# A SwiGLU trunk on one core: the forms of x moved beside the second chunk, and every sum of weight quarters on VectorE

## The chip, the cores and the metric

The kernel runs on one core of a Trainium2 chip. The metric is device time in microseconds (us), the median of several runs. A profiled execution of the kernel is there beside the times; its records show what each engine did and when.

## The reference

Two layers, 256 tokens, width 1024, inner width of an FFN 2816, all in float32. What matters here is the FFN, of which there are four (two in each layer); between them stand a mixer of three attention branches and a small gated input.

```python
def swiglu(x, w1, w3, w2):
    return (jax.nn.silu(x @ w1) * (x @ w3)) @ w2
...
    for i in range(DEPTH):
        h = h + 0.5 * swiglu(rms_norm(h, g_ffn1[i]), w1_a[i], w3_a[i], w2_a[i])
        u = rms_norm(h, g_mix[i])
        h = h + hybrid_mixer(u, w_in[i], ...)
        h = h + 0.5 * swiglu(rms_norm(h, g_ffn2[i]), w1_b[i], w3_b[i], w2_b[i])
        ple_gate = jax.nn.sigmoid(rms_norm(h, g_ple[i]) @ w_ple_gate[i])
        h = h + ple_gate * (p[i] @ w_ple_proj[i])
    return rms_norm(h, g_final)
```

## The kernel before

**Arithmetic.** TensorE multiplies operands in a rounded float32 form. Each float32 tile is therefore split into a rounded part "hi" and the rest "lo": ScalarE casts the hi part (line 135 for a tile, line 86 in `load`), VectorE subtracts it from the tile to get lo (lines 136 and 87), and each product is three matmuls, hi by hi, lo by hi and hi by lo (`mm3`, lines 102 to 104). In an FFN a weight tile is 128x1024 (512 KB), and a matmul of it is 128x128 by 128x512. So each tile of weights costs one cast on ScalarE and one subtraction on VectorE before TensorE can start on it.

**An FFN.** The inner width is cut into 11 chunks of 256 columns of w1 and 256 of w3. `up(c)` makes a chunk for both blocks of 128 tokens (`tb`), with 48 matmuls; `gated` turns the result into silu(x w1)*(x w3), a tile `pr` of 128x256 (ScalarE makes `act`, VectorE multiplies, line 238); `turn(c)` transposes `pr` on TensorE into `ffT` (fhi, flo); `down(c, j)` multiplies it with w2 into four banks `acc`. Chunks 0 and 1 are made first. Chunks 2, 3 and 4 are made in quarters (`up_unit`), spread between other work. Chunks 5 to 10 are made in pairs, (5,6), (7,8) and (9,10).

**A pair.** A pair is a product of a matrix of 2x2 blocks of x with one of 2x2 blocks of weights, made from seven block products in the place of eight. For that it needs sums of the blocks of x and sums of the blocks of weights:

- `x_forms`, once in an FFN: VectorE adds hi and lo of the four blocks of x (line 293), scales the second token block with `rb` (line 297; `rb` is a ratio of the two norms, brought to all partitions by a matmul with ones, line 274, and copied by ScalarE, line 276), makes the sums (lines 284 and 305) and splits five of them (tiles `q`). That is 15 VectorE operations of 128x512 beside three small ones.
- `pair(c)`: the four weight quarters x, y, w, z, each two tiles `wr` of 128x1024 that `fetch` loads through SyncE's queue. `form(i)` makes the sums in place: x+=w, x+=z and y+=x by VectorE (`add`, line 330), w+=z by an accumulating transfer that GpSimd issues and that reads z again from memory (`plus`, line 334). `make(i)` splits a quarter or a sum. `products()` yields the seven products in the order 1, 2, 5, 3, 6, 7, 4, each of 12 matmuls, with VectorE's sums of the results between (line 356, names m, u, v and c); a product has a bank `tr` of the two that there are, and the next product that wants the bank waits until it has been read.

`block` runs a plan: "S" is one product of the pair (with the splits and sums that the next ones need), "P" a quarter of an ordinary chunk, "D" a unit of `down`, "T" a `turn`. While one pair runs, the next pair's quarters are fetched, and its first product's tiles are split.

**Order.** A scheduler puts the instructions in order when the kernel is built; every engine then runs its own queue strictly in order, and waits at an instruction whose operands are late, with all that stands behind it. Before the change, the beginning of an FFN is written as up(0), up(1), then `x_forms`, the fetches of pair (5,6), turn(0), the splits for product 1 and the pair's plan, which begins with product 1. The first FFN differs: its first chunk is loaded together with x, and its norms are computed while chunk 1 runs.

Of the kernel before, what the change touches and what calls it, by code (L numbers as in the profile page):

```python
# [11 lines left out]
ALU = mybir.AluOpType  # L12
PSUM = bass.MemoryType.PSUM

P = 128
L = 2
S = 256
TB = S // P
D = 1024
# [14 lines left out]
def trunk(ctx: ExitStack, tc: tile.TileContext, a: dict, out: bass.AP):  # L34
    nc = tc.nc
# [13 lines left out]
    def const(name, shape):  # L49
        t = cp.tile(shape, F32, tag=name, name=name)  # L50
        tc.keep_in_program_order(nc.sync.dma_start(t, a[name]))
        return t
# [22 lines left out]
    def load(src, n=U, pool=None, step=U):  # L75
        raw = wp.tile([P, U], F32, tag="raw", name=nm("raw"), bufs=4)
        if pool is None:
            hi = wp.tile([P, U], F32R, tag="whi", name=nm("whi"), bufs=7)
            lo = wp.tile([P, U], F32R, tag="wlo", name=nm("wlo"), bufs=7)
        else:  # L80
            hi = pool.tile([P, U], F32R, tag="whi", name=nm("whi"), bufs=4)
            lo = pool.tile([P, U], F32R, tag="wlo", name=nm("wlo"), bufs=4)
        for i in range(0, n, step):
            c = slice(i, min(i + step, n))
            nc.sync.dma_start(raw[:, c], src[:, c])
            A.copy(hi[:, c], raw[:, c])  # L86
            V.tensor_tensor(out=lo[:, c], in0=raw[:, c], in1=hi[:, c].bitcast(F32), op=ALU.subtract)  # L87
        return hi, lo
# [26 lines left out]
    def bank_acc():  # L115
        return bank("acc", 4)
# [74 lines left out]
    def ffn(li, w13, w2, r, g, first=False, aside=None):  # L191
        nonlocal ident
        with tc.tile_pool(name=nm("fp"), bufs=3) as fp:
# [7 lines left out]
            if first:  # L201
                un0 = start(wtile)
            acc = []
            ffT = {}
            prs = {}

            def up(c, un, bank):
                os = []
                for tb in range(TB):
                    o = bank()  # L210
                    for kt in range(KT):
                        w = [x[:, (kt % 2) * 512 : (kt % 2) * 512 + 512] for x in un[kt // 2]]
                        mm3(o, x_at(tb, kt), w, kt == 0, kt == KT - 1)
                        if kt == 1:
                            settle()
                    os.append(o)
                    if r is not None:
                        gated(c, tb, o, r[tb])
                return os


# [12 lines left out]
            def gated(c, tb, o, scale):  # L234
                act = fp.tile([P, FC], F32, tag="act", name=nm("act"), bufs=2)
                A.activation(act, o[:, :FC], AF.Silu, scale=scale)
                pr = fp.tile([P, FC], F32, tag="pr", name=nm("pr"), bufs=6)
                V.scalar_tensor_tensor(
                    out=pr, in0=o[:, FC:], scalar=scale, in1=act, op0=ALU.mult, op1=ALU.mult
                )  # L240
                prs[c, tb] = pr

            def turn(c):
                fhi = fp.tile([P, 2, S], F32R, tag="fhi", name=nm("fhi"), bufs=4)
                flo = fp.tile([P, 2, S], F32R, tag="flo", name=nm("flo"), bufs=4)
                ffT[c] = (fhi, flo)
                t = bank_tr()
                for tb in range(TB):
                    for j in range(2):
                        PE.transpose(  # L250
                            t[:, j * S + tb * P : j * S + (tb + 1) * P], prs[c, tb][:, j * P : (j + 1) * P], ident
                        )
                split_T(t.rearrange("p (j t) -> p j t", j=2), fhi, flo)
# [61 lines left out]
            def pair(c, bank):  # L315
                t = {q: [wtile() for _ in range(2)] for q in "xywz"}
                fw = {}
                quarters = {"x": (0, 0), "y": (1, 0), "w": (0, 1), "z": (1, 1)}

                def at(q, u):  # L320
                    kh, nh = quarters[q]
                    return w13[li, c + nh, 2 * kh + u]

                def fetch(q):
                    for u in range(2):
                        nc.sync.dma_start(t[q][u], at(q, u))

                def add(q, other):
                    for u in range(2):
                        V.tensor_tensor(out=t[q][u], in0=t[q][u], in1=t[other][u], op=ALU.add)  # L330

                def plus(q, other):
                    for u in range(2):
                        nc.gpsimd.dma_start(t[q][u], at(other, u), accum_op=ALU.add)


                def form(i):
                    if i == 1:
                        add("x", "w")
                    elif i == 2:  # L340
                        add("x", "z")
                    elif i == 3:
                        plus("w", "z")
                    else:
                        add("y", "x")

                def make(i):
                    fw[i] = [split_w(w) for w in t[{1: "x", 2: "y", 5: "x", 3: "z", 6: "x", 7: "w", 4: "y"}[i]]]

                def product(o, i, start=False):  # L350
                    for kt in range(4):
                        m = [y[:, (kt % 2) * 512 : (kt % 2) * 512 + 512] for y in fw[i][kt // 2]]
                        mm3(o, [y[:, kt, :] for y in fx[i]], m, start and kt == 0, kt == 3, skip_group_check=True)

                def sum_(out, a, b, op=ALU.add):
                    V.tensor_tensor(out=out, in0=a, in1=b, op=op)


                def products():
                    o = bank()  # L360
                    product(o, 1, True)
                    m1 = t512("m1")
                    A.copy(m1, o)
                    yield
                    product(o, 2)
                    gated(c, 0, o, r[0])
                    yield
                    o = bank()
                    product(o, 5, True)
                    c5 = t512("c5")  # L370
                    A.copy(c5, o)
                    yield
                    product(o, 3)
                    v = t512("v")
                    A.copy(v, o)
                    yield
                    o = bank()
                    product(o, 6, True)
                    u2 = t512("u2")
                    sum_(u2, o, m1)  # L380
                    sum_(v, v, u2, ALU.subtract)
                    gated(c + 1, 0, v, r[0])
                    yield
                    product(o, 7)
                    sum_(m1, o, m1)
                    sum_(c5, c5, m1, ALU.subtract)
                    gated(c + 1, 1, c5, r[0])
                    yield
                    o = bank()
                    product(o, 4, True)  # L390
                    sum_(m1, o, m1)
                    gated(c, 1, m1, r[0])
                    yield

                return make, fetch, form, products()


# [33 lines left out]
                        turn(*arg)  # L431
                return following

            for c in range(2):
                if first and c == 1:

                    un = []
                    for i in range(4):
                        un.append(load(w13[li, c, i]))
                        if i < 2:  # L440
                            load_h(i)
                    ident = const("ident", [P, P])
                    r = [norm_r(tb) for tb in range(TB)]
                    for tb, o in enumerate(os0):
                        gated(0, tb, o, r[tb])
                    up(c, un, bank_acc)
                else:
                    os0 = up(c, un0 if first and c == 0 else [load(w13[li, c, i]) for i in range(4)], bank_mm)
                if c == 1:
                    acc.extend(bank_acc() for _ in range(4))  # L450
                    fx = x_forms()
                    wg = pair(5, bank_tr)
                    for q in "xywz":
                        wg[1](q)
                if c >= 1:
                    turn(c - 1)
            wg[0](1)
            if first:
                later()
            wg = block(wg, [  # L460
                ("S",), ("P", 2, 0), ("D", 0, 0), ("S",), ("P", 2, 1), ("S",), ("D", 0, 1), ("P", 2, 2), ("S",),
                ("T", 1), ("P", 2, 3), ("S",), ("D", 1, 0), ("S",), ("D", 1, 1), ("S",), ("T", 2),
            ], (7, bank_tr))
            wg = block(wg, [
# [576 lines left out]
    def load_h(tb):  # L1041
        tc.keep_in_program_order(nc.sync.dma_start(h[tb], a["x"][tb * P : (tb + 1) * P, :]))
# [8 lines left out]
    r = None  # L1051
    for li in range(L):
        g = [gcol[:, li, j, :] for j in range(4)]
        r = ffn(li, a["w13a"], a["w2a"], r, g[1], first=li == 0)
# [90 lines left out]
```

## Time and profile before

| what | value |
|---|---|
| median of 3 runs | 1357.7 us (1357.37 to 1358.7) |
| the profiled execution, its own time | 1355.51 us |
| its span in the trace | 1353.7 us |
| mean granted TensorE clock | 0.985 |
| TensorE (PE) busy | 1308.6 us, 97% of the span |
| VectorE (DVE) busy | 1042.0 us, 77% |
| ScalarE (ACT) busy | 837.2 us, 62% |
| GpSimd (POOL) busy | 69.5 us, 5% |

PEld in the profile is TensorE's loading of weights, which runs beside its matmuls. SPq and POOLq are the queues from which SyncE and GpSimd issue transfers. A row of a timeline gives a start, a duration, the engine, the line of the kernel, the operation, what it writes and reads, the shape, how many instructions lie in the row, and in brackets how long the engine had been idle and what ended that. The four FFNs begin at about 15, 460, 680 and 1130 us of the span, and run for some 180 us each.

### The profile page before, as it was taken

The page shows a single profiled execution, that of the slowest core. Times are in us where ns is not written, and L with a number is a line of the kernel's source. Part 1 is how long each engine was busy: PE and PEld are TensorE (multiplying, and loading weights), DVE is VectorE, ACT ScalarE, POOL GpSimd, SP SyncE. Part 2 cuts the span into 40 slices and gives each one's busy share as a digit, 9 for nine tenths or more (in the row PEclk, how much of TensorE's full clock was granted, in tenths as well). Part 3 has the DMA queues.
Part 4 walks back from the last instruction along what each step waited for, and adds up shares of the span by engine and source line. Part 5 has one row for each costly group of instructions (what it writes and reads, how often), then busy time and mean ns, then how long its engine had stood idle before and what let it go on. Part 6 is the DMA issues. An engine that isn't in the chain of part 4 may idle for free.

```text
span 1353.7 us, 18041 instructions
## 1 busy us (share of the span) xinstructions
PE 1308.6 (97%) x6576; PEld 1093.2 (81%) x6576; DVE 1042.0 (77%) x1466; ACT 837.2 (62%) x1257; POOL 69.5 (5%) x133
## 2 busy tenths in 40 slices
PE   8899999999999979999979999999999999799997
PEld 6688889978888858888858888898888788688886
DVE  6998875666768689897769988666666675998875
ACT  5666556665775456665746666566667744666655
POOL 1000000001100000000100000000010000000000
PEclk9899999999999989999999999999999999899999
DMA  8975457433546568555568744473444466675552
GB/s 306 314 251 156 139 164 222 167 125 126 169 143 186 190 211 276 187 147 180 170 219 273 234 121 150 147 225 134 156 145 136 157 187 241 210 236 160 155 169 81
DMA packets 71225, 249.21 MB, mean 184 GB/s; under 512 B 8544, under 2 KB 9184, under 8 KB 71136
## 3 DMA queue, kind: packets, MB, share of 16 engines
q1 hardware_dynamic: 67104, 234.39, 51.1%
q0 software_dynamic: 3456, 12.58, 5.5%
q8 instruction: 51, 0.84, 0.2%
q10 hardware_dynamic: 576, 1.08, 0.2%
q14 instruction: 38, 0.31, 0.1%
HBM read 246.98 MB, written 1.05 MB: 183 GB/s over the span
## 4 chain that ended last, share of the span: by engine, by line
PE 91%; DVE 5%; issue 1%; ACT 1%; DMA 1%; SPq 0%; POOLq 0%; POOL 0%; ACTq 0%
PE mm L102 15%; PE mm L104 14%; PE mm L103 14%; PE acc L103 8%; PE acc L104 8%; PE acc L102 8%; PE tr L103 6%; PE tr L102 5%; PE tr L104 5%; PE tr L250 1%; PE tr L150 1%; DVE q L136 1%; DVE wlo L136 1%; PE tr L742 1%; DVE wlo L87 1%
## 5 line engine op out<-in xcount | busy, mean ns | idle before, releaser
L87 DVE TENSOR_TENSOR wlo<-raw,whi 128x1024 fp32r<-128x1024 f32 (+1 forms) x346 | 411.4, 1200 | 93.1 <-ACT whi L86 90.8
L86 ACT CAST whi<-raw 128x1024 fp32r<-128x1024 f32 (+1 forms) x346 | 354.3, 1033 | 165.7 <-PE acc L104 52.3
L102 PE MATMUL mm<-whi,xhi 128*128 128x512 f32 (+1 forms) x632 | 247.1, 396 | 0.0
L104 PE MATMUL mm<-whi,xlo 128*128 128x512 f32 (+1 forms) x632 | 245.8, 389 | 0.0
L103 PE MATMUL mm<-wlo,xhi 128*128 128x512 f32 (+1 forms) x632 | 245.6, 389 | 0.0
L135 ACT CAST whi<-wr 128x1024 fp32r<-128x1024 f32 (+1 forms) x176 | 179.9, 1032 | 93.2 <-PE acc L104 53.1
L136 DVE TENSOR_TENSOR wlo<-wr,whi 128x1024 fp32r<-128x1024 f32 (+1 forms) x176 | 207.4, 1198 | 25.7 <-ACT whi L135 24.5
L104 PEld LDWEIGHTS mm<-whi,xlo 128*128 128x128 f32 x632 | 118.7, 188 | 24.8 <-DVE xlo L136 0.7
L102 PEld LDWEIGHTS mm<-whi,xhi 128*128 128x128 f32 x632 | 118.7, 188 | 24.4 <-DVE sqk L542 0.7
L104 PE MATMUL acc<-whi,flo 128*128 128x512 f32 x352 | 137.6, 391 | 0.0
L103 PEld LDWEIGHTS mm<-wlo,xhi 128*128 128x128 f32 x632 | 118.9, 188 | 23.1 <-DVE wlo L136 0.2
L103 PE MATMUL acc<-wlo,fhi 128*128 128x512 f32 x352 | 137.1, 390 | 0.0
L102 PE MATMUL acc<-whi,fhi 128*128 128x512 f32 x352 | 135.2, 392 | 0.0
L102 PE MATMUL tr<-whi,q 128*128 128x512 f32 x240 | 94.1, 392 | 0.0
L104 PE MATMUL tr<-whi,q 128*128 128x512 f32 x240 | 93.6, 390 | 0.0
L103 PE MATMUL tr<-wlo,q 128*128 128x512 f32 x240 | 93.4, 389 | 0.0
L330 DVE TENSOR_TENSOR wr<-wr,wr 128x1024 f32<-128x1024 f32 x72 | 86.3, 1222 | 0.0
L104 PEld LDWEIGHTS acc<-whi,flo 128*128 128x128 f32 x352 | 66.1, 188 | 13.8
L103 PEld LDWEIGHTS acc<-wlo,fhi 128*128 128x128 f32 x352 | 66.1, 188 | 13.5
L102 PEld LDWEIGHTS acc<-whi,fhi 128*128 128x128 f32 x352 | 66.1, 188 | 13.4
L102 PE MATMUL tr<-whi,xhi 128*128 128x512 f32 x96 | 42.3, 440 | 33.0 <-ACT whi L135 32.3
L102 PE MATMUL mm<-xhi,whi 128*128 128x256 f32 x256 | 73.8, 288 | 0.0
(253 smaller groups left out, 2169.0 us busy)
## 6 DMA issues: line engine op xcount, KB each, us to landing
wr<-in_w13a SPq DMA_DIRECT2D x48, 512.0 KB, 6.2
raw<-in_wg SPq DMA_DIRECT2D x48, 512.0 KB, 3.8
wr<-in_w13b SPq DMA_DIRECT2D x48, 512.0 KB, 5.8
raw<-in_w2a SPq DMA_DIRECT2D x44, 512.0 KB, 4.4
raw<-in_w2b SPq DMA_DIRECT2D x44, 512.0 KB, 4.3
raw<-in_w13b SPq DMA_DIRECT2D x40, 512.0 KB, 4.3
raw<-in_w13a SPq DMA_DIRECT2D x36, 512.0 KB, 4.6
raw<-in_wqk SPq DMA_DIRECT2D x32, 512.0 KB, 3.8
```

The source lines that it names most:

```text
L86: A.copy(hi[:, c], raw[:, c])
L87: V.tensor_tensor(out=lo[:, c], in0=raw[:, c], in1=hi[:, c].bitcast(F32), op=ALU.subtract)
L102: PE.matmul(o, lhs[0], rhs[0], start=first, stop=False, **more)
L103: PE.matmul(o, lhs[0], rhs[1], start=False, stop=False, **more)
L104: PE.matmul(o, lhs[1], rhs[0], start=False, stop=last, **more)
L135: A.copy(hi, t)
L136: V.tensor_tensor(out=lo, in0=t, in1=hi.bitcast(F32), op=ALU.subtract)
L150: PE.transpose(t[:, j * P : (j + 1) * P], h[tb][:, k * P : (k + 1) * P], ident)
L250: PE.transpose(t[:, j * S + tb * P : j * S + (tb + 1) * P], prs[c, tb][:, j * P : (j + 1) * P], ident)
L330: V.tensor_tensor(out=t[q][u], in0=t[q][u], in1=t[other][u], op=ALU.add)
L742: PE.transpose(t[:, j * P : (j + 1) * P], e[:, j * P : (j + 1) * P], ident)
```

## The change

1. In the FFNs after the first, `x_forms` stands between up(0) and up(1), and the quarters x, y and w of pair (5,6) are fetched between the loads of chunk 1; z follows up(1). In the first FFN the x, y and w fetches stand ahead of up(1), and `x_forms` is called within up(1), after its first token block.
2. The first plan begins with a quarter of chunk 2 ("P", 2, 0) and then product 1, not the other way round.
3. w+=z is an `add` on VectorE as the other three sums are. That takes 24 accumulating transfers of 512 KB (two in each of the 12 pairs) out of GpSimd's queue, and puts 24 additions of 128x1024 on VectorE.

```diff
-            def up(c, un, bank):
+            def up(c, un, bank, then=None):
...
+                    if tb == 0 and then is not None:
+                        then()
...
-                def plus(q, other):
-                    for u in range(2):
-                        nc.gpsimd.dma_start(t[q][u], at(other, u), accum_op=ALU.add)
...
-                        plus("w", "z")
+                        add("w", "z")
...
-                if c == 1:
-                    acc.extend(bank_acc() for _ in range(4))
-                    fx = x_forms()
-                    wg = pair(5, bank_tr)
-                    for q in "xywz":
-                        wg[1](q)
-                if c >= 1:
-                    turn(c - 1)
+            def begin():
+                nonlocal fx
+                fx = x_forms()
...
+            os0 = up(0, un0 if first else [load(w13[li, 0, i]) for i in range(4)], bank_mm)
+            wg = pair(5, bank_tr)
+            un = []
+            for i in range(4):
+                un.append(load(w13[li, 1, i]))
+                if first and i < 2:
+                    load_h(i)
+                if not first and i > 0:
+                    wg[1]("xyw"[i - 1])
+            if first:
...
+                for q in "xyw":
+                    wg[1](q)
+                up(1, un, bank_acc, begin)
+            else:
+                begin()
+                up(1, un, bank_mm)
+            wg[1]("z")
+            acc.extend(bank_acc() for _ in range(4))
+            turn(0)
             wg[0](1)
             if first:
                 later()
             wg = block(wg, [
-                ("S",), ("P", 2, 0), ("D", 0, 0), ("S",), ("P", 2, 1), ("S",), ("D", 0, 1), ("P", 2, 2), ("S",),
+                ("P", 2, 0), ("S",), ("D", 0, 0), ("S",), ("P", 2, 1), ("S",), ("D", 0, 1), ("P", 2, 2), ("S",),
```

The built program shows where the instructions went. In the rows below a name's number tells one buffer from another, and the line numbers of the changed kernel are two higher (L240 for L238, L286 for L284, L299 for L297, L332 for L330).

VectorE's queue at the start of the second FFN, before. The row ahead of these is the last gated tile of chunk 1; `flo` belongs to turn(0), and the last row is the lo part of the first weight tile of product 1:

```order
L297 TENSOR_TENSOR wr_4666<-wr_4666,rb_4664 128x512 x2
L136 TENSOR_TENSOR flo_4716<-tr_4717,fhi_4715 128x512
L284 TENSOR_TENSOR wr_4668<-wr_4666 128x512
L284 TENSOR_TENSOR wr_4666<-wr_4667,wr_4666 128x512
L136 TENSOR_TENSOR q_4677<-wr_4668,q_4676 128x512
L284 TENSOR_TENSOR wr_4668<-wr_4668,wr_4667 128x512
L305 TENSOR_TENSOR wr_4667<-wr_4667,wr_4668 128x512
L136 TENSOR_TENSOR q_4682<-wr_4668,q_4681 128x512
L136 TENSOR_TENSOR q_4687<-wr_4666,q_4686 128x512
L136 TENSOR_TENSOR q_4692<-wr_4667,q_4691 128x512
L136 TENSOR_TENSOR q_4696<-wr_4666,q_4695 128x512
L136 TENSOR_TENSOR wlo_4725<-wr_4699,whi_4724 128x1024
```

The same place after. wlo_4725 and wlo_4729 are the first two weight tiles of product 1; pr_4569 is the second gated tile of chunk 0, pr_4678 the first of chunk 1:

```order
L136 TENSOR_TENSOR wlo_4725<-wr_4571,whi_4724 128x1024
L136 TENSOR_TENSOR wlo_4729<-wr_4572,whi_4728 128x1024
L240 SCALAR_TENSOR_TENSOR pr_4569<-mm_4542,r_4461,act_4567 128x256
L299 TENSOR_TENSOR wr_4618<-wr_4618,rb_4616 128x512 x2
L87 TENSOR_TENSOR wlo_4734<-raw_4732,whi_4733 128x1024
L286 TENSOR_TENSOR wr_4620<-wr_4618 128x512
L332 TENSOR_TENSOR wr_4571<-wr_4571,wr_4575 128x1024
L136 TENSOR_TENSOR q_4629<-wr_4620,q_4628 128x512
L286 TENSOR_TENSOR wr_4618<-wr_4619,wr_4618 128x512
L286 TENSOR_TENSOR wr_4620<-wr_4620,wr_4619 128x512
L240 SCALAR_TENSOR_TENSOR pr_4678<-mm_4651,r_4406,act_4676 128x256
```

The lo parts for product 1 and the scaling by rb stood behind the last gated tile of chunk 1, and now stand around the last one of chunk 0, a whole up(1) earlier in the queue.

TensorE's queue at the end of up(1) in the second FFN, before (tr_4662 is the matmul that makes rb, tr_4717 is turn(0), tr_4742 product 1):

```order
L103 MATMUL mm_4624<-wlo_4591,xhi 128x512
L104 MATMUL mm_4624<-whi_4590,xlo 128x512
L274 MATMUL tr_4662<-xg_4660,ones 128x128
L250 MATMUL tr_4717<-ident,pr_4540 128x128 x2
L250 MATMUL tr_4717<-ident,pr_4569 128x128 x2
L102 MATMUL tr_4742<-whi_4724,xhi 128x512
L103 MATMUL tr_4742<-wlo_4725,xhi 128x512
```

The same place after (mm_4680 is the end of up(1), mm_4738 the quarter of chunk 2):

```order
L103 MATMUL mm_4680<-wlo_4603,xhi 128x512
L104 MATMUL mm_4680<-whi_4602,xlo 128x512
L252 MATMUL tr_4717<-ident,pr_4540 128x128 x2
L252 MATMUL tr_4717<-ident,pr_4569 128x128 x2
L102 MATMUL mm_4738<-whi_4733,xhi 128x512
L103 MATMUL mm_4738<-wlo_4734,xhi 128x512
```

Behind turn(0) comes the quarter of chunk 2, and product 1's matmuls follow among its; the matmul that makes rb has left this place and stands at the end of up(0), before the first matmul of up(1).

VectorE's queue in the first FFN, after (pr_301 and pr_372 are the gated tiles of chunk 1, line 295 is the addition of hi and lo in `x_forms`, wlo_390 and wlo_394 are product 1's weight tiles, wlo_419 is the quarter of chunk 2):

```order
L136 TENSOR_TENSOR wlo_390<-wr_202,whi_389 128x1024
L136 TENSOR_TENSOR wlo_394<-wr_203,whi_393 128x1024
L240 SCALAR_TENSOR_TENSOR pr_301<-acc_274,r_247,act_299 128x256
L240 SCALAR_TENSOR_TENSOR pr_372<-acc_345,r_258,act_370 128x256
L295 TENSOR_TENSOR wr_312<-xhi,xlo 128x512 x2
L299 TENSOR_TENSOR wr_312<-wr_312,rb_310 128x512 x2
L295 TENSOR_TENSOR wr_313<-xhi,xlo 128x512 x2
L286 TENSOR_TENSOR wr_314<-wr_312 128x512
L136 TENSOR_TENSOR flo_381<-tr_382,fhi_380 128x512
L286 TENSOR_TENSOR wr_312<-wr_313,wr_312 128x512
L136 TENSOR_TENSOR q_323<-wr_314,q_322 128x512
L87 TENSOR_TENSOR wlo_419<-raw_417,whi_418 128x1024
```

Here the scheduler left all of `x_forms` behind the last gated tile of chunk 1, as before, and only product 1's two lo parts came ahead of it. In the third FFN the additions of line 295 likewise follow the second gated tile of chunk 0; the fourth is like the second. Between the FFNs (the mixers, the gated inputs) the queues hold the same rows in the same order.

More of the change, by code (lines that the diff above doesn't have):

```diff
@@ L432, in block @@
                 return following
[L434 to L448, printed above, removed]
-                if c == 1:
-                    acc.extend(bank_acc() for _ in range(4))
-                    fx = x_forms()
-                    wg = pair(5, bank_tr)
-                    for q in "xywz":
-                        wg[1](q)
-                if c >= 1:
-                    turn(c - 1)
+            def begin():
+                nonlocal fx
+                fx = x_forms()
+            fx = None
+            os0 = up(0, un0 if first else [load(w13[li, 0, i]) for i in range(4)], bank_mm)
[8 more added lines that the diff above has]
+            if first:
+                ident = const("ident", [P, P])
+                r = [norm_r(tb) for tb in range(TB)]
+                for tb, o in enumerate(os0):
+                    gated(0, tb, o, r[tb])
+                for q in "xyw":
[7 more added lines that the diff above has]
+            turn(0)
             wg[0](1)
```

## The prediction

> **What bounds the kernel.** I read the page's busy times and chain first, to see which engine sets the end.
>
> ```profile
> PE 1308.6 (97%) x6576; PEld 1093.2 (81%) x6576; DVE 1042.0 (77%) x1466; ACT 837.2 (62%) x1257; POOL 69.5 (5%) x133
> PE 91%; DVE 5%; issue 1%; ACT 1%; DMA 1%; SPq 0%; POOLq 0%; POOL 0%; ACTq 0%
> ```
>
> TensorE is busy for all but 1353.7 - 1308.6 = 45.1 us. So the second view is what TensorE waits for.
>
> ```profile
> PE tr L102 <- ACT whi L135: 32.3, 4, 8.1
> PE tr L103 <- DVE wlo L136: 1.9, 4, 0.5
> PE tr L102 <- DVE m L356: 0.7, 3, 0.2
> ```
>
> Four waits of 8.1 us are 32.3 of the 45.1 us: one at each FFN's product 1. The timeline of TensorE shows the second FFN's.
>
> ```profile
> 479.56 0.60 PE L250 MATMUL tr<-ident,pr 128*128 128x128 f32 x4
> 488.24 0.79 PE L102 MATMUL tr<-whi,xhi 128*128 128x512 f32 x1 [8.09 <-ACT whi L135]
> 489.50 0.79 PE L103 MATMUL tr<-wlo,xhi 128*128 128x512 f32 x1 [0.47 <-DVE wlo L136]
> 490.52 0.63 PE L102 MATMUL tr<-whi,xhi 128*128 128x512 f32 x1
> 490.95 0.63 PE L103 MATMUL tr<-wlo,xhi 128*128 128x512 f32 x1
> 493.93 0.39 PE L104 MATMUL tr<-whi,xlo 128*128 128x512 f32 x1
> 494.16 0.63 PE L102 MATMUL mm<-whi,xhi 128*128 128x512 f32 x2
> ```
>
> The wait is not the whole loss. After it the matmuls start 0.43 us apart (490.52, 490.95), and only from 493.93 on 0.23 apart. Turn(0) ends at about 480.0; twelve matmuls at 0.2275 would end at 482.7, and they end at 494.16. Each FFN's beginning thus loses about 11.4 us on TensorE: 8.1 of wait, about 1 for the lo part, the rest slow matmuls.
>
> Third, VectorE across the same place, and its busy time by stage.
>
> ```profile
> 474.60 0.48 DVE L238 SCALAR_TENSOR_TENSOR pr<-mm,r,act 128x256 f32<-128x256 f32 x1 [4.90 <-ACT act L236]
> 480.04 0.48 DVE L238 SCALAR_TENSOR_TENSOR pr<-mm,r,act 128x256 f32<-128x256 f32 x1 [4.96 <-ACT act L236]
> 480.44 1.28 DVE L297 TENSOR_TENSOR wr<-wr,rb 128x512 f32<-128x512 f32 x2
> 481.64 0.69 DVE L136 TENSOR_TENSOR flo<-tr,fhi 128x512 fp32r<-128x512 f32 x1
> ...
> 485.72 2.50 DVE L136 TENSOR_TENSOR q<-wr,q 128x512 fp32r<-128x512 f32 x4
> 488.23 4.63 DVE L136 TENSOR_TENSOR wlo<-wr,whi 128x1024 fp32r<-128x1024 f32 x4
> 492.77 2.36 DVE L330 TENSOR_TENSOR wr<-wr,wr 128x1024 f32<-128x1024 f32 x2
> 495.04 2.36 DVE L87 TENSOR_TENSOR wlo<-raw,whi 128x1024 fp32r<-128x1024 f32 x2
> ```
>
> ```profile
> 441.00:450.00 9.00, 9.00 (x41) 7.43 (x40) 4.33 (x6) 2.61 (x4) 0.19 (x1) 1.00 0.36 125
> 29.00:39.20 10.20, 1.65 (x9) 0.88 (x7) 9.35 (x15) 6.28 (x11) 0.00 (x0) 0.70 1.00 399
> 462.70:479.00 16.30, 16.30 (x74) 13.49 (x73) 6.10 (x13) 4.27 (x6) 0.00 (x0) 1.00 0.81 299
> 479.00:490.00 11.00, 2.44 (x11) 1.62 (x10) 9.85 (x15) 6.77 (x12) 0.00 (x0) 0.71 0.42 154
> 490.00:535.00 45.00, 44.77 (x193) 36.46 (x193) 43.93 (x45) 31.46 (x38) 3.54 (x4) 0.96 0.75 246
> 535.00:645.00 110.00, 110.00 (x506) 90.80 (x505) 91.77 (x99) 65.32 (x81) 2.73 (x5) 1.00 0.56 172
> ```
>
> (Columns: stretch, length, busy PE, PEld, DVE, ACT, POOL, then TensorE's granted clock, DMA share, GB/s.) VectorE is idle during up(1), waiting twice about 4.9 us for gated tiles, and then does the forms of x (480.44 to 488.23) while TensorE stands still. From 479 to 535 it has hardly a pause: TensorE leads the whole kernel, but through pair (5,6) VectorE follows close behind, and that decides how much of the gap can be had.
>
> **How much VectorE allows.** From the rows above, start to start, an operation of 128x1024 takes 1.135 us (492.77 to 495.04, two), one of 128x512 takes 0.60 (480.44 to 481.64, two), one of 128x256 takes 0.40 (480.04 to 480.44). The pair ends for TensorE when VectorE has read the result of product 4: the next pair's first product waits for that bank. I take that read as the mark.
>
> ```profile
> 29.74 0.48 DVE L238 SCALAR_TENSOR_TENSOR pr<-acc,r,act 128x256 f32<-128x256 f32 x1 [1.56 <-ACT act L236]
> 82.55 0.69 DVE L356 TENSOR_TENSOR m<-tr,m 128x512 f32<-128x512 f32 x1
> 462.74 0.16 DVE L269 RECIPROCAL rho<-r 128x1 f32<-128x1 f32 x1
> 533.33 0.68 DVE L356 TENSOR_TENSOR m<-tr,m 128x512 f32<-128x512 f32 x1
> 534.07 0.50 PE L102 MATMUL tr<-whi,xhi 128*128 128x512 f32 x1 [0.23 <-DVE m L356]
> 689.79 0.48 DVE L238 SCALAR_TENSOR_TENSOR pr<-mm,r,act 128x256 f32<-128x256 f32 x1 [1.34 <-ACT act L236]
> 752.63 0.68 DVE L356 TENSOR_TENSOR m<-tr,m 128x512 f32<-128x512 f32 x1
> 1132.75 0.16 DVE L269 RECIPROCAL rho<-r 128x1 f32<-128x1 f32 x1
> 1202.89 0.69 DVE L356 TENSOR_TENSOR m<-tr,m 128x512 f32<-128x512 f32 x1
> ```
>
> In the new queue of the second FFN there stand, from the reciprocal (462.74) to that read, 37 operations of 128x1024, 22 of 128x512, 9 of 128x256 and three tiny ones: 42.0 + 13.2 + 3.6 + 0.3 = 59.1 us. With no pause at all the read ends at 521.9, against 534.0 before: 12.1 us at most, more than the 11.4 that TensorE has lost. The same count for the fourth FFN (from 1132.75) ends at 1191.9 against 1203.5: at most 11.6. In the third the additions of hi and lo stand behind the gated tile of 689.79; from there 32, 22 and 8 operations are 52.7 us, end 742.5 against 753.2: at most 10.7. In the first everything but product 1's lo parts still stands behind the tile of 29.74; 31, 22 and 6 are 50.8 us, end 80.5 against 83.15: at most 2.6. So the order moves much in three FFNs and little in the first.
>
> **The change, part by part.** I followed the new queues of TensorE, VectorE and ScalarE row by row with these durations, each row starting at the later of its queue's predecessor and its operands.
>
> - *Forms of x ahead of up(1), second and fourth FFN.* VectorE is then busy from 462.7 on; the quarters x, y, w are fetched in the places of SyncE's queue that fell at about 441 to 450, where transfers fill 0.36. When up(1) ends at 479.6, product 1's weights are split and the forms nearly so. Turn(0), the quarter of chunk 2 and product 1, 24 matmuls, run through from 480.0 to 485.4. The wait of 8.1 us and its slow matmuls are gone. Next late is the lo part for D(0,0), at about 486.1: 0.7 us; two more such waits of 0.2. Product 3 ends at 505.4 against 515.9, 10.5 earlier. At the pair's end VectorE's read is about 0.6 us further behind TensorE than now. Net 9.8 us each, against caps of 11.4.
> - *The third FFN.* VectorE must idle some 4 us before 689.79, and ScalarE's copy of rb, which waits for the end of up(0), holds up a cast behind it. I find one wait of about 2 us at product 2, and 8.0 us net, under the cap of 10.7.
> - *The first FFN.* Product 1 runs at once after up(1), but the quarter of chunk 2 then waits for its cast, which stands behind the forms on ScalarE: 3.4 us; then 2 and 1 us more. The work on VectorE is what it was, so the gain can only come from its pauses: 1.5 us, between 0 and the cap of 2.6.
> - *w+=z on VectorE.* The sums of quarters that VectorE makes now, and the queue of the accumulating transfers:
>
> ```profile
> L330 DVE TENSOR_TENSOR wr<-wr,wr 128x1024 f32<-128x1024 f32 x72 | 86.3, 1222 | 0.0
> q0 software_dynamic: 3456, 12.58, 5.5%
> ```
>
>   24 x 1.135 = 27.2 us more work. In the first pair of each FFN the 2.27 us are in the counts above. In the other eight pairs VectorE's pauses cover them: 535 to 645 holds two pairs, VectorE is busy 91.77 of 110 us, and 4.54 more leave 13.7. The pauses lie behind w+=z in the pair, so the delay is gone before the bank's read:
>
> ```profile
> 555.04 1.23 DVE L87 TENSOR_TENSOR wlo<-raw,whi 128x1024 fp32r<-128x1024 f32 x1 [0.61 <-ACT whi L86]
> 557.32 1.23 DVE L87 TENSOR_TENSOR wlo<-raw,whi 128x1024 fp32r<-128x1024 f32 x1 [1.05 <-ACT whi L86]
> 560.49 2.59 DVE L136 TENSOR_TENSOR wlo<-wr,whi 128x1024 fp32r<-128x1024 f32 x2 [1.34 <-ACT whi L135]
> ```
>
>   These three alone are 3.0 us, more than 2.27. I take 0; without the cover it would be up to 8 x 2.27 = 18.2 us.
> - *The accumulating transfers go.* 12.58 MB leave the GpSimd queue. Transfers fill 0.56 to 0.75 of the stretches above and TensorE waits for none there, so 0; the lower end is the 0.23 us waits, the upper nothing that I can find.
>
> Sum: 9.8 + 8.0 + 9.8 + 1.5 = 29.1 us off the profiled execution's 1355.5, so 1326.4; the median stood 2.2 above that execution, so 1328.6, rounded to 1329.
>
> A rule of the skill bears on the slow matmuls. The row first: after the 8.09 us wait the matmuls were 0.43 apart for some 5 us and the stretch's granted clock was 0.71. The Trainium skill, "TensorE: Matmul & The Clock Gate", section "Part 1: The HAM clock gate", says that an idle window of about 3.4 us halves the clock until as long a busy one has passed; this trace agrees in kind (0.43 against 0.23). By that rule the first FFN's new wait of 3.4 us lies just at the edge and may bring a slow stretch back. My own price for a slow stretch there is the row's: 12 matmuls at 0.43 in place of 0.23 are 2.4 us, which takes the first FFN's 1.5 to -0.9 and the sum to 1331; that is the third rival.
>
> **The rivals.**
>
> *All that the caps allow.* The small waits of my walk don't come: 2.6 + 11.4 + 10.7 + 11.4 = 36.1 us, time 1321.6. For it: TensorE's own present waits inside a pair are only 0.2 to 0.5 us. Against: VectorE was busy 43.93 of 45 us there, so each late cast passes on.
>
> *VectorE is the limit and gives half.* Rows moved into up(1) wait at queue heads (rb, a cast, a quarter still in flight) more than I found, about 5 us in each of three FFNs: 29 - 15 = 14 us, time 1343. For it: the third FFN shows such a loss already.
>
> *The slow clock returns* where new waits stand, in the first and the third FFN: 1331 to 1334.
>
> *Slower.* VectorE's queue sticks at L299, the first row that needs rb. In the profile rb comes only after up(1). If it came as late again, nothing would be pulled ahead, the gap would stay, and each FFN's first pair would carry 2.27 us more: 1357.7 + 9.1 = 1366.8. It decides from a stall of 12 us on, rb at about 482 where my walk has it at 470. Against it: the matmul that makes rb now stands before up(1) in TensorE's queue.
>
> *No change* would need the caps to be wrong by their whole size; I see no mechanism.
>
> **How the numbers follow.** Chances: the forecast (1324 to 1333) 0.48, all the caps (1318 to 1324) 0.12, slow clock 0.10, half (1334 to 1350) 0.20, slower 0.06, within 0.2% 0.04. A change of 0.2%, 2.7 us, is about the least that a measurement of this kernel tells from none. The range leaves out the rare cases and the far half of the fourth: low is the caps with 3 us for what the counts leave out, 1318, high the half gain, 1343. Faster 0.90, same 0.04, slower 0.06.
>
> **What the new profile would show.** The wait of product 1 for the cast gone from the list of TensorE's waits in three FFNs; TensorE busy at nearly the same sum in a span shorter by 29 us; VectorE's pauses in 463 to 479 filled; 96 additions of weight quarters, up from 72, and the software queue absent; in the first FFN waits of some us behind up(1) in the place of the 8.1. I am wrong if the gaps come back elsewhere in the pair, or if the eight later pairs show new waits of TensorE for VectorE.

## The result, and the profile after

| | before | after |
|---|---|---|
| median of 3 runs | 1357.7 us (1357.37 to 1358.7) | 1320.02 us (1319.48 to 1322.45) |
| profiled execution, its own time | 1355.51 us | 1320.02 us |
| span | 1353.7 us | 1318.2 us |
| mean granted TensorE clock | 0.985 | 0.998 |

The ratio is 0.9726 (95% interval 0.9703 to 0.9748): 37.7 us faster, where 29 were forecast, inside the range and below the likeliest case's own band. The page after, its busy times, its chain and the sums of quarters (the software queue is no longer listed):

```profile
PE 1301.7 (99%) x6576; PEld 1087.2 (82%) x6576; DVE 1064.3 (81%) x1490; ACT 836.4 (63%) x1257; POOL 45.3 (3%) x109
PE 93%; DVE 5%; ACT 1%; issue 1%; DMA 0%; POOLq 0%; POOL 0%; ACTq 0%; DVEq 0%
L332 DVE TENSOR_TENSOR wr<-wr,wr 128x1024 f32<-128x1024 f32 x96 | 113.7, 1219 | 0.0
```

TensorE's 45.1 us outside its busy time have become 1318.2 - 1301.7 = 16.5, and its busy time itself has lost 6.9 us. That fits the slow matmuls that are gone: in the second FFN before the change the granted clock was 0.51 from 488 to 494, and from 459 to 530 it is 1.00 now. Its waits after:

```profile
PE mm L102 <- ACT whi L86: 3.7, 1, 3.7
PE tr L102 <- ACT whi L135: 1.1, 2, 0.9
PE tr L102 <- DVE m L354: 1.0, 2, 0.5
```

The four waits of 8.1 us are gone, and one of 3.7 us has come, in the first FFN. In the second FFN TensorE goes from turn(0) into the quarter of chunk 2 with one wait of 0.30 us:

```profile
475.61 0.60 PE L252 MATMUL tr<-ident,pr 128*128 128x128 f32 x4
475.96 0.48 PE L102 MATMUL mm<-whi,xhi 128*128 128x512 f32 x1
478.82 0.50 PE L102 MATMUL mm<-whi,xhi 128*128 128x512 f32 x1 [0.30 <-DVE pr L240]
```

To see where the gain was made, the first update of h in each FFN serves as a mark. The rows of VectorE before, then after:

```profile
187.84 0.69 DVE L486 SCALAR_TENSOR_TENSOR h<-acc,h 128x512 f32<-128x512 f32 x1 [0.41 <-PE acc L104]
638.61 0.69 DVE L486 SCALAR_TENSOR_TENSOR h<-acc,h 128x512 f32<-128x512 f32 x1 [0.41 <-PE acc L104]
857.91 0.69 DVE L486 SCALAR_TENSOR_TENSOR h<-acc,h 128x512 f32<-128x512 f32 x1 [0.41 <-PE acc L104]
1308.19 0.69 DVE L486 SCALAR_TENSOR_TENSOR h<-acc,h 128x512 f32<-128x512 f32 x1 [0.41 <-PE acc L104]
```

```profile
183.90 0.69 DVE L491 SCALAR_TENSOR_TENSOR h<-acc,h 128x512 f32<-128x512 f32 x1 [0.41 <-PE acc L104]
624.13 0.69 DVE L491 SCALAR_TENSOR_TENSOR h<-acc,h 128x512 f32<-128x512 f32 x1 [0.41 <-PE acc L104]
833.37 0.69 DVE L491 SCALAR_TENSOR_TENSOR h<-acc,h 128x512 f32<-128x512 f32 x1 [0.41 <-PE acc L104]
1272.97 0.69 DVE L491 SCALAR_TENSOR_TENSOR h<-acc,h 128x512 f32<-128x512 f32 x1 [0.41 <-PE acc L104]
```

From mark to mark the gains are 3.94, 10.54, 10.06 and 10.68 us, and 0.3 behind the last: 35.5 us of span. The other 2.2 us of the median's 37.7 lie between the runs: before, the profiled execution was 2.2 us quicker than its median, after it is the median.

### The profile page after: what moved, and what is told of

Its sections match the earlier page's. It is cut to its first block, busy times and chain, and to the rows that moved or that the text cites. A ratio compares the mean times of both kernels' runs of the same rounds, so it can differ in the third digit from the quotient of the medians.

```text
span 1318.2 us, 17958 instructions
## 1 busy us (share of the span) xinstructions
PE 1301.7 (99%) x6576; PEld 1087.2 (82%) x6576; DVE 1064.3 (81%) x1490; ACT 836.4 (63%) x1257; POOL 45.3 (3%) x109
## 4 chain that ended last, share of the span: by engine, by line
PE 93%; DVE 5%; ACT 1%; issue 1%; DMA 0%; POOLq 0%; POOL 0%; ACTq 0%; DVEq 0%
PE mm L102 15%; PE mm L104 14%; PE mm L103 14%; PE acc L103 8%; PE acc L104 8%; PE acc L102 8%; PE tr L102 5%; PE tr L104 5%; PE tr L103 5%; PE tr L252 1%; PE tr L150 1%; DVE wlo L87 1%; PE tr L747 1%; DVE wlo L136 1%; PE acc L849 1%
## 5 line engine op out<-in xcount | busy, mean ns | idle before, releaser
L332 DVE TENSOR_TENSOR wr<-wr,wr 128x1024 f32<-128x1024 f32 x96 | 113.7, 1219 | 0.0
L104 PE MATMUL mm<-xhi,wlo 128*128 128x256 f32 x256 | 72.4, 283 | 0.0
```

Of the source, the lines that this page charges most:

```text
L104: PE.matmul(o, lhs[1], rhs[0], start=False, stop=last, **more)
```

## The experiments

The theory when they began, A: a VectorE that idles in up(1) and is then the limit; work pulled into the pause is what counts; in the first pair of an FFN VectorE has no room left, in later pairs it has. The rivals are the additions themselves (B), VectorE as the limit everywhere (C), and the new plan. Medians, and ratios to the kernel before on the same chip:

| kernel | median, us | ratio (95%) |
|---|---|---|
| a0_again | 1320.66 | 0.9738 (0.9722 to 0.9755) |
| e1_plus_back | 1319.24 | 0.9726 (0.9711 to 0.9741) |
| e2_adds_only | 1357.67 | 1.0010 (1.0000 to 1.0019) |
| e11_S_first | 1322.05 | 0.9749 (0.9731 to 0.9767) |
| e3_more_later | 1322.50 | 0.9747 (0.9732 to 0.9761) |
| e4_more_first | 1323.94 | 0.9760 (0.9746 to 0.9775) |
| e9_forms_late | 1320.09 | 0.9731 (0.9717 to 0.9746) |
| e10_fetch_late | 1320.17 | 0.9733 (0.9717 to 0.9749) |
| e12_both_late | 1353.34 | 0.9974 (0.9965 to 0.9983) |
| e14_P_first_only | 1355.67 | 0.9999 (0.9989 to 1.0008) |
| e8_sums_early | 1324.52 | 0.9775 (0.9759 to 0.9791) |
| e13_sums_early_plus | 1320.67 | 0.9742 (0.9728 to 0.9757) |

**a0_again.** The changed kernel unchanged.

> The changed kernel once more, as the base for the others on this chip. Every theory expects 1320 us within 2.

It measured 1320.66.

**Where the 33 us come from.** Three kernels undo, in the second to fourth FFN, one half of the new beginning, the other half, and both.

e9_forms_late:

```diff
             else:
-                begin()
                 up(1, un, bank_mm)
+                begin()
```

> The changed kernel with x_forms behind up(1) again in the second, third and fourth FFN; the early fetches, the early split of product 1 and the new plan stay. Theory A (what counts is VectorE's work pulled into its pauses of up(1)): the 11 operations of 0.6 us from the scaling on come back behind up(1), 6.6 us for each of three FFNs less what the early lo parts still fill, 8 to 20 us slower. Rival (only product 1's weights had to come early, since the first products that need the forms come later): within 2 us of the changed kernel.

e10_fetch_late:

```diff
-                if not first and i > 0:
-                    wg[1]("xyw"[i - 1])
...
+            if not first:
+                for q in "xyw":
+                    wg[1](q)
             wg[1]("z")
```

> The changed kernel with the quarters x, y, w fetched behind up(1)'s loads, as before the change, in the second, third and fourth FFN; x_forms stays ahead of up(1). Theory A: VectorE still does the forms within up(1), the quarters land only near its end, and the lo parts and first sums (about 5 operations of 1.135 us) are pushed behind it: 3 to 10 us slower. Rival (the forms alone were the gap): within 1.5 us. Rival (the late weights alone were the gap): 8 us and more in each of three FFNs, over 24 us.

e12_both_late has both of these edits.

> The changed kernel with both x_forms and the fetches of x, y, w behind up(1) again in the second, third and fourth FFN; the new plan and the additions stay. Either one late cost nothing, since VectorE's pauses in up(1) then took the other's work. Theory D (it doesn't matter which work fills the pauses, only that some is there): now none is, the pause of 10 us comes back, and 8 to 11 us in each of three FFNs, 1345 to 1352. Rival (the new plan, the quarter of chunk 2 ahead of product 1, is what covers the wait): within 5 us of the changed kernel, 1320 to 1325.

Either half alone cost nothing (1320.09 and 1320.17); both together cost 33 us (1353.34, or 11 us in each of three FFNs). The stretch of up(1) in the second FFN shows why. The rows are, in turn, the changed kernel, e9, e10 and e12; the third busy number is VectorE's:

```profile
459.00:475.50 16.50, 16.50 (x75) 13.69 (x75) 15.65 (x24) 11.64 (x17) 0.00 (x0) 1.00 0.59 207
...
459.00:476.00 17.00, 17.00 (x79) 14.15 (x78) 14.52 (x21) 10.50 (x13) 0.00 (x0) 1.00 0.37 110
...
459.00:476.00 17.00, 17.00 (x79) 14.05 (x78) 15.48 (x27) 10.51 (x16) 0.00 (x0) 1.00 0.83 311
...
459.00:476.00 17.00, 17.00 (x77) 14.08 (x76) 6.57 (x13) 4.27 (x6) 0.00 (x0) 1.00 0.81 301
```

In e9 the lo parts and sums of the pair fill VectorE's pause, in e10 the forms of x and then product 1's lo parts do; in both VectorE is busy for some 15 of 17 us. In e12 nothing fills it (6.57 us; the kernel before has 6.10 between 462.7 and 479), and the old wait is back in three FFNs, 8.1 us in each:

```profile
PE tr L102 <- ACT whi L135: 25.2, 5, 8.1
```

So theory A's numbers for e9 and e10 were wrong. What held is that work had to come into VectorE's idle 10 us; which work, the queue of ScalarE shows. The wait of product 1 ends with ScalarE's cast of its first weight tile. The rows are, in turn, the kernel before, e9 and e10, all in the second FFN:

```profile
485.07 2.18 ACT L135 CAST q<-wr 128x512 fp32r<-128x512 f32 x4 [1.49 <-DVE wr L284]
487.15 3.88 ACT L135 CAST whi<-wr 128x1024 fp32r<-128x1024 f32 x4
...
462.14 1.06 ACT L135 CAST whi<-wr 128x1024 fp32r<-128x1024 f32 x1
...
470.06 2.18 ACT L135 CAST q<-wr 128x512 fp32r<-128x512 f32 x4 [1.48 <-DVE wr L286]
472.52 1.99 ACT L135 CAST whi<-wr 128x1024 fp32r<-128x1024 f32 x2
```

Before, and in e12, that cast stands behind the five casts of the forms (`q`), which wait for VectorE's sums, and the sums came only after up(1). In e9 it stands ahead of the forms; in e10 the forms are done, so it follows them. In both it falls within up(1), whose end is turn(0) at 475.77 and 475.86, and neither has a wait for it between 458 and 490. The forms that e9 makes after up(1) are first needed at 487.58. So the rivals of e9 and e10 are both half right: product 1's split has to be done by the end of up(1), and for that either it goes ahead of the forms or the forms come early too; neither half is the only way. Two things no run shows: whether any other work in the pause would do (none was put there, and by these rows it would leave the cast where it was), and what is gained by only putting the split ahead of the forms, with both left behind up(1).

e14_P_first_only, the kernel before with the new first plan, and e11_S_first, the changed kernel with the old one:

```diff
-                ("S",), ("P", 2, 0), ("D", 0, 0), ("S",), ("P", 2, 1), ...
+                ("P", 2, 0), ("S",), ("D", 0, 0), ("S",), ("P", 2, 1), ...
```

> The kernel before with only the new plan (the quarter of chunk 2 ahead of product 1). Theory D: the quarter's lo part stands behind the same forms in VectorE's queue or covers at most 12 matmuls, 2.7 us in each of four FFNs: 1346 to 1357. Rival (the plan is the cause): under 1335.

> The changed kernel with the old first plan: product 1 ahead of the quarter of chunk 2. Theory A: product 1's weights are split before up(1) ends, so the order of the two is worth nothing: within 1.5 us of the changed kernel. Rival: the quarter of chunk 2 is what covers product 1's wait; without it 2.7 to 5 us in each of three FFNs, 8 to 15 us slower.

The plan alone is worth nothing (ratio 0.9999), and without it the changed kernel is 1.4 us slower in the medians, within the intervals of the ratios. The rival that the quarter covers the wait is out: in e14, as in the kernel before, the 8.1 us waits stand four times.

**The additions.** e1_plus_back puts w+=z back on accumulating transfers in the changed kernel, e2_adds_only makes additions of them in the kernel before:

```diff
-                        plus("w", "z")
+                        add("w", "z")
```

(e2; e1 is the reverse.)

> The changed kernel with w+=z by accumulating transfers again: 24 additions of 1.135 us leave VectorE, nothing else is moved. Theory A (in a first pair VectorE closely limits TensorE, in later pairs its pauses cover the additions): 1 to 4 us faster than the changed kernel, most of it in the first FFN, where VectorE has no pause (2 x 1.135 = 2.3 us). Theory B (the additions on VectorE are part of what brought the gain, since the transfers were late or in the way): slower by several us. Theory C (VectorE is the limit in all pairs): up to 27 us faster.

> The kernel before with w+=z as additions on VectorE and nothing else changed. Theory A: the first pair of each FFN, where VectorE has hardly a pause, takes 2.3 us more, the later ones nothing: 1357.7 + 5 to 9 = 1363 to 1367. Theory B: faster than 1357.7. Theory C: 1357.7 + 27 = 1385. If the additions are free everywhere: 1358.

e1 is 1.4 us faster than a0 in the medians, and the intervals of the ratios overlap; e2 is 1.0 us slower than before, where A expected 5 to 9. Theories B and C are out: the additions brought nothing, and cost 1.0 to 1.4 us in the medians, about as much as these runs can tell. Why A missed shows in VectorE's queue at the end of the second FFN's first pair. Before, two sums for the next pair stood ahead of the read that frees the bank (the row at 533.33); in e2 they follow it:

```profile
525.96 1.22 DVE L330 TENSOR_TENSOR wr<-wr,wr 128x1024 f32<-128x1024 f32 x1
532.20 1.22 DVE L330 TENSOR_TENSOR wr<-wr,wr 128x1024 f32<-128x1024 f32 x1
```

```profile
534.02 0.68 DVE L356 TENSOR_TENSOR m<-tr,m 128x512 f32<-128x512 f32 x1
534.72 0.69 DVE L136 TENSOR_TENSOR flo<-tr,fhi 128x512 fp32r<-128x512 f32 x1
535.34 0.48 DVE L238 SCALAR_TENSOR_TENSOR pr<-m,r,act 128x256 f32<-128x256 f32 x1
535.74 2.35 DVE L330 TENSOR_TENSOR wr<-wr,wr 128x1024 f32<-128x1024 f32 x2
```

Two additions came in ahead of that read, and the scheduler moved two others behind it. By the marks e2 loses 0.6, 0.1, 1.3 and 0.6 us in the four FFNs, where A expected 2.3 in each. What "has no room" in one order had room for most of the 2.27 us in another.

e3_more_later and e4_more_first double the suspected cost:

```diff
                         add("w", "z")
+                        if c > 5:                        # e4: if c == 5
+                            for u in range(2):
+                                V.tensor_tensor(out=t["w"][u], in0=t["w"][u], in1=t["w"][u], op=ALU.max)
```

> The changed kernel with two more VectorE operations of 128x1024 (the larger of a tile and itself, the result unchanged) behind w+=z in each of the eight later pairs: 16 x 1.135 = 18.2 us more on VectorE. Theory A (pauses behind w+=z cover it there): 0 to 2 us slower than the changed kernel. Theory C (VectorE limits all pairs): 18 us slower.

> The same two extra operations, but only in the first pair of each FFN: 8 x 1.135 = 9.1 us more on VectorE, half of what the later pairs were given. Theory A (in the first pair VectorE has no room left): 6 to 9 us slower than the changed kernel, though it is half the work. If VectorE has room there too: under 1 us.

18.2 us of extra work in the later pairs cost 1.8 us against a0; half as much in the first pairs cost 3.3, where A expected 6 to 9. The order of the two is as A said, and C is out again, but the first pairs are not full. By the marks, e4's loss against a0 is 1.9 us in the first FFN and then -1.0, 1.1 and -0.1, and e3's is 1.2 in the first FFN and -0.9, -0.1 and -0.6 in the others. The changed kernel's own two profiles (the first one and a0's) differ by 0.7, 0.5, 0.0 and 0.9 us between the same marks, so only e4's 1.9 in the first FFN stands clear of that.

**The first FFN.** e8_sums_early calls the four additions of hi and lo, which the changed kernel leaves behind up(1) there, early (`x_sums`, ahead of the norms); e13_sums_early_plus also has the accumulating transfers of e1.

```diff
+            if first:
+                pre = x_sums()
             wg = pair(5, bank_tr)
```

> The changed kernel with the four additions of hi and lo in the first FFN early in VectorE's queue, between the splits of x and of chunk 1, where the kernel before had three of them. Theory E (in the kernel before, GpSimd's small operation for the norm took 3.3 us because VectorE ran one operation with two operands from memory after another): GpSimd's operation is long again, or moved with the gap between VectorE's, and up(1)'s end slips by 1 to 2 us. Theory F (in the first FFN VectorE is the limit up to the pair's end): the 2.4 us of additions leave the stretch behind up(1), and the FFN ends 1 to 3 us earlier. Both together: -2 to +1 us against the changed kernel. If neither holds: 0, and GpSimd's operation stays at 0.3 us.

> The same, and w+=z by accumulating transfers again in all pairs, so that VectorE has the least to do: the best of the pieces together. Theory F: the gain of the two pieces adds, 2 to 4 us faster than the changed kernel, 1316 to 1318. If TensorE alone is the limit by now: within 1.5 us of the changed kernel.

e8 is 3.9 us slower than a0 (1324.52), outside the -2 to +1 expected, and e13 no faster (1320.67): theory F's gain did not come, and no piece or pair of pieces beat the changed kernel by more than the intervals. By its mark e8 ends the first FFN at 187.62, 3.7 us behind the changed kernel. TensorE's waits in e8 show a longer one in the place of the 3.7 us, and a new one:

```profile
PE mm L102 <- ACT whi L86: 5.6, 1, 5.6
PE mm L103 <- DVE wlo L87: 2.6, 1, 2.6
```

With the additions out of the way the scheduler put four sums of weights ahead of the lo part of chunk 2's quarter, for which TensorE waits. That e13, with two of the four sums gone from VectorE, loses the second wait fits this; whether a better order in the first FFN gains anything was not tried. Theory E held. GpSimd's small operation for the norm before, in the changed kernel and in e8:

```profile
15.22 3.32 POOL L171 TENSOR_SCALAR ss<-ss 128x1 f32<-128x1 f32 x1 [14.26 <-ACT junk L164]
...
15.01 0.31 POOL L171 TENSOR_SCALAR ss<-ss 128x1 f32<-128x1 f32 x1 [14.05 <-ACT junk L164]
...
14.79 3.40 POOL L171 TENSOR_SCALAR ss<-ss 128x1 f32<-128x1 f32 x1 [13.84 <-ACT junk L164]
```

and VectorE beside it before:

```profile
14.92 0.69 DVE L293 TENSOR_TENSOR wr<-xhi,xlo 128x512 f32<-128x512 f32 x1
15.52 1.23 DVE L87 TENSOR_TENSOR wlo<-raw,whi 128x1024 fp32r<-128x1024 f32 x1
16.66 0.70 DVE L293 TENSOR_TENSOR wr<-xhi,xlo 128x512 f32<-128x512 f32 x1
17.26 1.23 DVE L87 TENSOR_TENSOR wlo<-raw,whi 128x1024 fp32r<-128x1024 f32 x1
20.08 0.48 DVE L238 SCALAR_TENSOR_TENSOR pr<-mm,r,act 128x256 f32<-128x256 f32 x1 [1.60 <-ACT act L236]
```

VectorE ran one operation on another until 18.48, and GpSimd's operation, one number per partition, ended at 18.54. Of the 14 profiles, the five with these additions early (before, e2, e14, e8, e13) have it at 3.32 to 3.41 us and turn(0) at 28.9 to 29.6; the other nine have it at 0.25 to 0.32 and turn(0) at 27.5 to 28.3. The means of turn(0) differ by 1.5 us. The way from the one to the other is ScalarE, which needs the norm for `act` (before, then after):

```profile
19.57 0.47 ACT L236 ACTIVATE act<-mm,r 128x256 f32<-128x256 f32 x1 [2.75 <-POOL r L175]
...
16.80 0.48 ACT L238 ACTIVATE act<-mm,r 128x256 f32<-128x256 f32 x1 [0.18 <-POOL r L175]
```

Behind `act` in its queue stand the casts of chunk 1's last weight tiles.

## Why the prediction was right, and where it was short

**Right.** The place (four waits of 8.1 us, one at each product 1), the loss of 11.4 us in each, and the reason (VectorE idle in up(1), then working while TensorE stands), though the link through ScalarE's queue, and that half of the move would do, were not seen. In three FFNs the limits held too: 11.4, 10.7 and 11.4 us against 10.54, 10.06 and 10.68. The 10.7 is from counting VectorE's queue; the two of 11.4 are what TensorE had lost, as the count allowed 12.1 and 11.6. The additions in the later pairs at nothing: 16 more operations cost 1.8 us. The additions and the transfers together at nothing: e1, which undoes both, lies within the intervals. Of the cases, the time lies in that of "all that the caps allow" (1318 to 1324, 0.12), not in the forecast's (0.48).

**Short by 6.4 us of the span's 35.5, and 2.2 of offset.** These terms were mis-sized:

- The third FFN, "one wait of about 2 us at product 2", 8.0 us; it measured 10.06. The walk had ScalarE's copy of rb wait for the end of up(0). The rows of TensorE and then ScalarE in the changed kernel show that rb's matmul stands earlier, within up(0), and that neither the copy nor the cast behind it waits; TensorE's only listed wait from 668 to 750 is one of 0.2 us:

```profile
671.83 0.38 PE L276 MATMUL tr<-xg,ones 128*128 128x128 f32 x2
```

```profile
672.97 0.26 ACT L278 COPY rb<-tr 128x128 f32<-128x128 f32 x1
673.18 1.05 ACT L135 CAST whi<-wr 128x1024 fp32r<-128x1024 f32 x1
674.61 0.48 ACT L238 ACTIVATE act<-mm,r 128x256 f32<-128x256 f32 x1 [0.38 <-PE mm L104]
```

- The first FFN, "the gain can only come from its pauses", 1.5 us and no more than 2.6; it measured 3.94. The cap was counted from the gated tile at 29.74, taken as fixed. That tile now comes at 28.30, as turn(0), the end of up(1), came 1.66 us earlier: the additions that had held up GpSimd, and with it the norm, `act` and chunk 1's split, had left that place. The move was not seen: the text ahead of the prediction has all of `x_forms` behind the last gated tile of chunk 1 "as before", but before the change its four additions ran from 10.12 to 17.36, far ahead of that tile, and only the rest stood behind it. The 2.28 us that remain lie under the cap.
- The second and fourth FFN, "0.7 us; two more such waits of 0.2", 9.8 us; they measured 10.54 and 10.68, with waits of 0.30 and 0.5 us in the second and of 0.5 in the fourth.
- The median, taken as 2.2 us above the profiled execution: that was this execution's luck, and the profile after is its median.

**The slow clock** of the third rival did come in the first FFN, one of the two places where it was put, and cost nothing that shows; in the third FFN there was no such wait, and the granted clock was 1.00 from 668 to 740. After the wait of 3.69 us in the first FFN the changed kernel's matmuls start 0.42 us apart, and 0.23 from 38.73 on:

```profile
30.57 0.39 PE L104 MATMUL tr<-whi,xlo 128*128 128x512 f32 x1
34.65 0.73 PE L102 MATMUL mm<-whi,xhi 128*128 128x512 f32 x2 [3.69 <-ACT whi L86]
35.59 0.80 PE L102 MATMUL tr<-whi,xhi 128*128 128x512 f32 x1 [0.22 <-ACT whi L135]
36.19 0.63 PE L103 MATMUL mm<-wlo,xhi 128*128 128x512 f32 x1
36.61 0.63 PE L104 MATMUL mm<-whi,xlo 128*128 128x512 f32 x1
...
38.73 0.40 PE L104 MATMUL mm<-whi,xlo 128*128 128x512 f32 x1
38.96 0.40 PE L102 MATMUL mm<-whi,xhi 128*128 128x512 f32 x1
...
31.00:39.00 8.00, 4.14 (x11) 3.00 (x12) 8.00 (x13) 6.55 (x10) 0.00 (x0) 0.79 0.81 256
```

VectorE was busy for all 8.00 us of that stretch, so without the slow matmuls TensorE would probably have waited a little further on; no run shows that. What the Trainium skill says in "TensorE: Matmul & The Clock Gate", section "Part 1: The HAM clock gate", that an idle window of about 3.4 us halves the clock, agrees with this trace: 3.69 us of idle time was enough, and so was 3.44 in e11.

## What to carry to other kernels

Where the leading engine waits once for a long preparation on others, look for their pause just ahead, and for what stands in their queues in front of the operand it waits for. Move either the operand's own preparation or what stands in front of it into the pause; here each half did it alone, and each was worth nothing beside the other, so undoing one part alone would have told that neither matters. Count the helper's queue between two marks: the count bounded three of the four gains within 1.6 us, while the walk through single waits missed by 0.7 to 2.4. Take no mark of such a count for fixed without asking what the move does ahead of it.

## What was not expected of the hardware

A GpSimd operation on 128x1 elements, 190 ns in the median of 18, took 3.32 to 3.41 us in the five kernels in which VectorE ran operations with two tensor operands without a pause beside it, and ended when VectorE paused. Spans on GpSimd are rough in these profiles, but ScalarE's wait of 2.75 us for the norm shows the same delay. The Trainium skill, "SBUF — State Buffer", section "SBUF: two separate sides", says that such a VectorE operation and a GpSimd operation that reads the same memory exclude each other for a whole instruction. The traces agree that GpSimd waits; they add that it waited through more than one VectorE instruction, until VectorE had a pause. Whether operations with one operand would let it pass was not tried.
